# Projecting q and k of one head ahead of a norm, and moving thirty weight subtractions from VectorE to GpSimd

## The chip, the cores and the metric

The kernel runs on one core of one Trainium2 chip. The metric is device time in microseconds (us) for one execution. The engines are TensorE (PE, its weight loads PEld), VectorE (DVE), ScalarE (ACT), GpSimd (POOL) and SyncE (SP), which only issues DMAs here; GpSimd issues some DMAs too.

## What is computed

A decoder trunk of two layers over 512 tokens of width 1024, all in fp32. The mixer runs an S5 state space model (four heads of it, as the kernel groups it) and retention (four heads) side by side, from one projection. Its head matters here:

```python
def rms_norm(x, g):
    xf = x.astype(jnp.float32)
    y = xf * lax.rsqrt(jnp.mean(xf * xf, axis=-1, keepdims=True) + EPS)
    return (y * g.astype(jnp.float32)).astype(x.dtype)
...
for l in range(DEPTH):
    h = rms_norm(x, norm_mix[l])
    proj = h @ w_in[l]
    u, q, k, v, g = jnp.split(proj, split_at, axis=-1)
    y_ssm = s5_mixer(u, ...)
    y_ssm = rms_norm(y_ssm, s5_out_norm[l])
    y_ret = retention(q, k, v, g, positions, ret_out_norm[l])
    x = x + jnp.concatenate([y_ssm, y_ret], axis=-1) @ w_out[l]
    ...
    x = x + memory_cross_attention(h, m, wq, wk, wv, wo)
    ...
    x = x + (jax.nn.silu(h @ w_gate) * (h @ w_up)) @ w_down
return rms_norm(x, norm_final)
```

The row scale of a norm commutes with the projection, so the kernel multiplies x times gain by the weights first and applies the scale (`nrm.bc`) when a result is taken out of PSUM.

## The kernel before

**Precision.** Every large matmul is done as three fp32r matmuls on high and low parts: `mm3` issues high x high, high x low, low x high. The activations' parts are `u_nmh` and `u_nml` in the first norm. Weights come in chunks of 128 x 1024 fp32. For a plain chunk (`prep_chunk`) SyncE loads `raw`, ScalarE copies it to the high part (`w<-raw`, rounded to fp32r), and VectorE writes the low part as raw minus high (`w<-raw,w`). For six chunks of q, k and g in layer 0 the low part is made without VectorE: ScalarE writes minus the high part, and a DMA on GpSimd's queue adds raw to it. Gate and up chunks of the feed-forward go another way (`prep_pair`) and are not touched.

**Order of the weights.** `chunk_order` lists all chunks in the order of their use; for a mixer these are u, then v, then what the string `PLAN[l]` names step by step: Q, K, G project q, k, g of a head; S and Y are the states and the output of an S5 head; C and P the scores and the weighted values of a retention head; M, L, V are memory keys, GLU and memory values; F ends retention. A chunk is prepared when the one four places before it is used (`LOOKAHEAD`); five `raw` and eight `w` buffers turn over.

**Order of the instructions.** The program is recorded first and placed by a list scheduler (`Program.due`, `Program.schedule`) that knows a price for each operation, gives each a due time from its users, and picks on each engine the ready operation with the earliest due time for which buffers are free. `EVAC` bounds how long a result may stay in PSUM before its due time. The result is one fixed order for each engine; all instructions are emitted from one line (L405, memsets from L403). An engine runs its order strictly in turn.

**The first norm (layer 0).** TensorE multiplies u0 and u1 from eight 128 x 256 weight pieces (`u_w0h`, `u_w0l`) as the input x arrives in eight tiles, then u2 and u3 from plain chunks. In the meantime ScalarE squares the tiles (`u_nmq`) and VectorE adds them up (`u_nma`). `nrm.root` then takes the column sum on TensorE (a 128 x 1 matmul, `ps<-c,u_nma`), the inverse root on VectorE, and the spread to all partitions on TensorE (128 x 128 with `ident`). Only then can u leave PSUM, times the scale. The v chunks follow, then `PLAN[0]`, which begins with Q0 K0 S0.

**GpSimd** does the S5 setup of layer 0 at the start (128 x 32 and 128 x 256 operations, ending in `u_s5bb`), clears some buffers with memsets, issues its DMAs and does the last scaling of the kernel. VectorE reads `u_s5bb` for the matrices of S0 (`u_mt`).

Of the kernel before, what the change touches and what calls it, by code (L numbers as in the profile page):

```python
# [38 lines left out]

PLAN = ("Q0 K0 S0 G0 C0 S1 Q1 K1 Y0 P0 S2 G1 Y1 C1 P1 S3 Q2 Y2 K2 Q3 K3 C2 G2 C3 Y3 P2 "  # L40
        "G3 M P3 F L V",
        "Q0 S0 K0 G0 C0 K1 S1 P0 Q1 Y0 G1 C1 S2 Q2 P1 Y1 K2 G2 C2 S3 Y2 Q3 K3 P2 G3 C3 "
        "P3 F M Y3 L V")
EPS = 1e-6
TWO_PI = 6.28318501
# [5 lines left out]

ADDED = ("q", "k", "g")
WARM = 8

# [20 lines left out]
def chunk_order():  # L75

    o = []
    for l in range(L):
        o += [("u", l, m) for m in range(4)]
        o += [("v", l, m) for m in range(4)]  # L80
        count = {"q": 1, "k": 1, "g": 1, "ck": KT, "glu": 2, "cv": 8}
        for step in PLAN[l].split():
            key = {"Q": "q", "K": "k", "G": "g", "M": "ck", "L": "glu", "V": "cv"}.get(step[0])
            if key:
                m = int(step[1:] or 0)
                o += [(key, l, m + i) for i in range(count[key])]
        o += [("out", l, m) for m in range(KT)]
        o += [("cq", l, m) for m in range(KT)]
        o += [("co", l, m) for m in range(KT)]
        for a, b in FPARTS[l]:  # L90
            for f in range(a, b, 2):
                o += [("gate", l, a, b, f), ("up", l, a, b, f)]
            o += [("down", l, f) for f in range(a, b)]
    return o
# [63 lines left out]
class Op:  # L158
    __slots__ = ("i", "prio", "eng", "fn", "args", "dur", "deps", "users", "wait", "ready", "end", "cap",
                 "bufs", "tab", "bytes", "rec")  # L160

# [44 lines left out]
class Program:  # L206
    def __init__(self, slots):
        self.ops, self.slots = [], slots
        self.cap, self.made = CAP, {}

# [9 lines left out]
    def add(self, eng, fn, k):  # L220
        o = Op()
        o.i = len(self.ops)
        o.cap = self.cap
        o.eng, o.fn, o.args = eng, fn, k
# [34 lines left out]
    def due(self):  # L259

        t = 0.0
        for o in self.ops:
            if o.eng == "PE":
                o.prio = t
                t += o.dur
            else:
                o.prio = o.rec = t
        for o in reversed(self.ops):
            if o.eng == "PE":
                o.prio = min([u.prio - o.dur - LEAD for u in o.users if u.eng != "PE"]  # L270
                             + [u.prio for u in o.users if u.eng == "PE"] + [o.prio])
                continue
            o.prio = min([u.prio - o.dur - LEAD for u in o.users] + [o.prio + o.cap])
            o.prio = max(o.prio, o.rec - EARLY)
            if o.bytes:
                o.prio = max(o.prio - AHEAD, FIRST)
            for d in o.deps:
                if d.eng == "PE":
                    o.prio = min(o.prio, d.prio + EVAC)

# [137 lines left out]
def trunk(ctx, tc, io):  # L418
# [48 lines left out]
    for kind in (3, 5):  # L467
        place.update((i, n) for n, i in enumerate(i for i, x in enumerate(order) if len(x) == kind))
    ready = {}
    state = {"prep": 0, "use": 0}  # L470
# [3 lines left out]
    def prep_chunk(i):  # L474
# [9 lines left out]
        else:  # L484
            V.tensor_tensor(out=lo, in0=raw, in1=hi.bitcast(F32), op=sub)
        ready[i] = (hi, lo)
# [150 lines left out]

    vec = load("vec", [P, NVEC])
    xs = [perm([P, SEQ], f"x{i}") for i in range(KT)]
    first = []  # L640
    for i in range(KT):
        Q.dma_start(out=xs[i], in_=io["xT"][:, i, :])
        raw, hi, lo = gen("w0")[:, :256], gen("w0h", F32R)[:, :256], gen("w0l", F32R)[:, :256]
        Q.dma_start(out=raw, in_=io["w"][i // 4, :, 256 * (i % 4):256 * (i % 4) + 256])
# [12 lines left out]
    gam = load("gam", [P, TT * HEADS])  # L657
    geps = load("geps", [P, SEQ])

# [72 lines left out]
    class Norm:  # L732
# [38 lines left out]

        def root(self, wide, scale=1.0):

# [9 lines left out]
            colsum(ps, self.acc, ones_d, nt)  # L783
            self.col = rsqrt(ps[:, :nt], nt, "nrm_col", None, scale)
            pb = bank(self.s + "bc")
            spread(pb, self.col, nt)
# [445 lines left out]

    def proj(key, l, m, nrm):
        ps = bank(key)
        w = chunk(key, l, m)
        for kt in range(KT):
            mm3(ps, cut(w, slice(None), slice(kt * P, (kt + 1) * P)), nrm.parts[kt],
                kt == 0, kt == KT - 1)
        return ps

# [45 lines left out]
    def ret_fin(stat, ys, outs):  # L1286

        m = gen("rm")
        V.tensor_tensor(out=m, in0=stat, in1=geps, op=add)
# [8 lines left out]
    def mixer(l, nrm, nxt, begin):  # L1298
# [12 lines left out]
        if l == 0:  # L1311
            begin()
            pu += [proj("u", l, m, nrm) for m in (2, 3)]
            for x in xs:
                nrm.stat(x)
        nrm.root(False)
        if l == 0:
            rotary()
        cr, sr = gen("cr"), gen("sr")
        V.tensor_tensor(out=cr, in0=rcos, in1=nrm.bc, op=mul)  # L1320
        V.tensor_tensor(out=sr, in0=rsin, in1=nrm.bc, op=mul)
        for m in range(4):
# [4 lines left out]
                            in1=by4(nrm.bc), op=mul)  # L1327
            us.append(u)
        if l == 0:
            selectors()  # L1330
        vs = ret_v(l, nrm)
        mats, sts, zs = {}, {}, {}
# [6 lines left out]

        q, k, p, pg = {}, {}, {}, {}  # L1340
        for step in PLAN[l].split():
# [477 lines left out]
```

## Time and profile before

| | |
|---|---|
| median of 3 runs | 1474.37 us (1473.48 to 1475.53) |
| the profiled execution | 1473.55 us |
| its span, first to last instruction | 1471.7 us |
| mean granted TensorE clock | 0.994 |
| TensorE busy | 1452.0 us, 99% of the span |
| VectorE busy | 1194.9 us, 81% |
| ScalarE busy | 798.8 us, 54% |
| GpSimd busy | 98.7 us, 7% |

Busy time is the sum of an engine's instructions, register and DMA-issuing ones left out. The span lies 1.85 us below the execution's time; the difference is what lies around the instructions. The granted clock is a share of full speed: 1.00 is 2.4 GHz, 0.50 is 1.2 GHz.

### The profile page before, as it was taken

Reading aid. Unit: us, or ns where it says so; the run is one execution under the profiler, and the core shown is the slowest. Engines: PE = TensorE matmul, PEld = TensorE weight load, DVE = VectorE, ACT = ScalarE, POOL = GpSimd, SP = SyncE. Lnnn points to the kernel's source line nnn. Section 1 sums busy time; section 2 is a strip of 40 time slices with the busy share of each in tenths; the row PEclk is TensorE's granted clock in tenths of the full one; section 3 lists DMA queues with packets and bytes.
Section 4 is the critical chain, followed back from the end, with each engine's and each line's share of the span. In section 5 each row is a group of like instructions: output and inputs, shape, how many; then the busy total and the mean of one; then the engine's idle time right before and its main releaser. Section 6 shows DMA issues by size and latency. Waiting matters only on the chain.

```text
span 1471.7 us, 23057 instructions
## 1 busy us (share of the span) xinstructions
PE 1452.0 (99%) x8784; PEld 1277.5 (87%) x8784; DVE 1194.9 (81%) x2078; ACT 798.8 (54%) x1375; POOL 98.7 (7%) x202
## 2 busy tenths in 40 slices
PE   8999999999999999999999999999999999999997
PEld 6888788888898998998988888888889989999897
DVE  8799996676899897897973989757679969869596
ACT  5887665344665464565645436544456636436264
POOL 5721000000000101002000000000000000000001
PEclk8999999999999999999999999999999999999999
DMA  7534534221134334244445553432121322413321
GB/s 254 158 87 105 177 131 154 100 72 51 50 115 149 118 119 151 87 143 156 137 139 170 157 165 115 144 129 87 58 72 57 116 101 87 145 59 127 101 87 58
DMA packets 67311, 172.47 MB, mean 117 GB/s; under 512 B 11264, under 2 KB 22912, under 8 KB 67200
## 3 DMA queue, kind: packets, MB, share of 16 engines
q1 hardware_dynamic: 64096, 160.51, 32.6%
q0 software_dynamic: 3104, 10.49, 2.5%
q8 instruction: 69, 1.13, 0.3%
q14 instruction: 42, 0.34, 0.1%
HBM read 156.55 MB, written 13.63 MB: 116 GB/s over the span
## 4 chain that ended last, share of the span: by engine, by line
PE 81%; DVE 13%; ACT 3%; issue 2%; DMA 0%; SPq 0%; DVEq 0%; ACTq 0%
PE ps L405 81%; DVE w L405 4%; DVE u_gs L405 1%; DVE u_us L405 1%; DVE raw L405 1%; ACT w L405 1%; DVE s L405 1%; DVE u_gw L405 0%; DMA x<-in_xT_dram 0%; ACT u_vc L405 0%; DVE u_actl L405 0%; ACT u_v L405 0%; SPq L405 0%; DVE u_ry L405 0%; DVE u_mt L405 0%
## 5 line engine op out<-in xcount | busy, mean ns | idle before, releaser
L405 ACT ACTIVATE w<-raw 128x1024 fp32r<-128x1024 f32 (+1 forms) x348 | 348.1, 1003 | 415.6 <-PE ps L405 341.6
L405 PE MATMUL ps<-u_nff,w 128*128 128x256 f32 x3696 | 438.6, 279 | 1.0 <-DVE w L405 1.0
L405 PEld LDWEIGHTS ps<-u_nff,w 128*128 128x128 f32 x3696 | 435.8, 188 | 4.4 <-DVE w L405 1.8
L405 DVE TENSOR_TENSOR w<-raw,w 128x1024 fp32r<-128x1024 f32 (+1 forms) x336 | 385.0, 1152 | 54.5 <-ACT w L405 54.1
L405 PE MATMUL ps<-u_acth,w 128*128 128x512 f32 (+1 forms) x768 | 224.1, 374 | 0.0
L405 PEld LDWEIGHTS ps<-u_acth,w 128*128 128x128 f32 x768 | 139.6, 188 | 25.3 <-ACT u_acth L405 0.4
L405 PE MATMUL ps<-u_nmh,w 128*128 128x512 f32 x480 | 158.3, 401 | 0.0
L405 PE MATMUL ps<-u_actl,w 128*128 128x512 f32 (+1 forms) x384 | 143.7, 376 | 1.4 <-DVE u_actl L405 1.2
L405 DVE TENSOR_TENSOR x<-ps,x 128x512 f32<-128x512 f32 x88 | 60.6, 690 | 99.4 <-PE ps L405 99.3
L405 PEld LDWEIGHTS ps<-u_nmh,w 128*128 128x128 f32 x480 | 91.1, 191 | 18.6
L405 PE MATMUL ps<-u_nml,w 128*128 128x512 f32 x240 | 95.4, 397 | 0.0
L405 PEld LDWEIGHTS ps<-u_actl,w 128*128 128x128 f32 x384 | 72.1, 188 | 17.1 <-DVE u_actl L405 3.9
L405 PE MATMUL ps<-u_nch,w 128*128 128x512 f32 x256 | 81.7, 393 | 0.0
L405 PE MATMUL ps<-u_xoh,w 128*128 128x512 f32 x256 | 80.7, 392 | 0.0
L405 DVE TENSOR_TENSOR raw<-raw 128x512 f32<-128x512 f32 x88 | 60.3, 685 | 5.3 <-DMA raw<-in_ws_dram 5.1
L405 DVE TENSOR_TENSOR raw<-raw,raw 128x512 f32<-128x512 f32 x88 | 60.3, 685 | 0.3
L405 DVE TENSOR_TENSOR u_gs<-u_gs,u_nfry 128x512 f32<-128x512 f32 x88 | 59.5, 689 | 0.3
L405 PEld LDWEIGHTS ps<-u_nch,w 128*128 128x128 f32 x256 | 48.1, 188 | 10.4
L405 POOL TENSOR_TENSOR u_fin<-u_lp,u_lbc 128x512 f32<-128x512 f32 x4 | 5.4, 1391 | 767.9 <-ACT u_lbc L405 767.9
L405 PEld LDWEIGHTS ps<-u_xoh,w 128*128 128x128 f32 x256 | 48.0, 188 | 9.9
L405 PEld LDWEIGHTS ps<-u_nml,w 128*128 128x128 f32 x240 | 45.7, 190 | 9.5
L405 PE MATMUL ps<-u_xol,w 128*128 128x512 f32 x128 | 50.4, 393 | 0.0
(368 smaller groups left out, 2472.2 us busy)
## 6 DMA issues: line engine op xcount, KB each, us to landing
raw<-in_w_dram SPq DMA_DIRECT2D x166, 512.0 KB, 3.4
raw<-in_ws_dram SPq DMA_DIRECT2D x88, 512.0 KB, 3.7
u_s5x<-sp SPq DMA_DIRECT2D x28, 256.0 KB, 4.2
w<-in_w_dram POOLq DMA_DIRECT2D x6, 512.0 KB, 6.3
u_mr<-in_memT_dram SPq DMA_DIRECT2D x12, 256.0 KB, 4.7
x<-in_xT_dram SPq DMA_DIRECT2D x8, 256.0 KB, 4.8
tu<-u_u SPq DMA_DIRECT2D x8, 256.0 KB, 3.8
u_ub<-tu SPq DMA_DIRECT2D x32, 64.0 KB, 3.5
```

What stands on the lines that cost most here:

```text
L405: getattr(engines[o.eng], o.fn)(**k)
```

## The change

1. `chunk_order` puts q and k of head 0 of layer 0 between u and v (`AHEAD_OF_NORM`), and `PLAN[0]` loses Q0 K0. In `mixer` the rotary tables are recorded earlier, then q0 is projected, then half of k0; `nrm.root` runs the second half of k0 between its column sum and its spread (`mid`). Both stay in PSUM until the u results are out, and are then rotated. `prog.evac` is 40000 while these steps are recorded and 4000 again after them.
2. `POOLED`: of the list of plain mixer chunks of a layer (u, v, q, k, g, ck, glu, cv: 38 of them), every second from number 13 in layer 0 and from number 4 in layer 1 gets its low part from GpSimd: 13 and 17 chunks.
3. A one-column Copy on ScalarE ahead of everything, and the load of `vec` behind the first tile of x.
4. `geps` is loaded where retention ends, into a passing buffer, and no longer at the start.

```diff
--- before.py
+++ after.py
@@ -37,10 +37,12 @@
 
 
 
-PLAN = ("Q0 K0 S0 G0 C0 S1 Q1 K1 Y0 P0 S2 G1 Y1 C1 P1 S3 Q2 Y2 K2 Q3 K3 C2 G2 C3 Y3 P2 "
+PLAN = ("S0 G0 C0 S1 Q1 K1 Y0 P0 S2 G1 Y1 C1 P1 S3 Q2 Y2 K2 Q3 K3 C2 G2 C3 Y3 P2 "
         "G3 M P3 F L V",
         "Q0 S0 K0 G0 C0 K1 S1 P0 Q1 Y0 G1 C1 S2 Q2 P1 Y1 K2 G2 C2 S3 Y2 Q3 K3 P2 G3 C3 "
         "P3 F M Y3 L V")
+
+AHEAD_OF_NORM = (("q", 0), ("k", 0))
 EPS = 1e-6
 TWO_PI = 6.28318501
 MAGIC = 12582912.0
@@ -50,6 +52,8 @@
 LOOKAHEAD = 4
 
 ADDED = ("q", "k", "g")
+
+POOLED = (13, 4)
 WARM = 8
 
 
@@ -77,6 +81,8 @@
     o = []
     for l in range(L):
         o += [("u", l, m) for m in range(4)]
+        if l == 0:
+            o += [(key, l, m) for key, m in AHEAD_OF_NORM]
         o += [("v", l, m) for m in range(4)]
         count = {"q": 1, "k": 1, "g": 1, "ck": KT, "glu": 2, "cv": 8}
         for step in PLAN[l].split():
@@ -157,7 +163,7 @@
 
 class Op:
     __slots__ = ("i", "prio", "eng", "fn", "args", "dur", "deps", "users", "wait", "ready", "end", "cap",
-                 "bufs", "tab", "bytes", "rec")
+                 "bufs", "tab", "bytes", "rec", "evac")
 
 
 LATENCY = {("PE", "PE"): 0, ("ACT", "ACT"): 0, ("DVE", "DVE"): 127, ("PE", "DVE"): 196,
@@ -206,7 +212,7 @@
 class Program:
     def __init__(self, slots):
         self.ops, self.slots = [], slots
-        self.cap, self.made = CAP, {}
+        self.cap, self.evac, self.made = CAP, EVAC, {}
 
     def buf(self, kind, s="", dt=None):
         b = Buf(kind, None, s)
@@ -220,7 +226,7 @@
     def add(self, eng, fn, k):
         o = Op()
         o.i = len(self.ops)
-        o.cap = self.cap
+        o.cap, o.evac = self.cap, self.evac
         o.eng, o.fn, o.args = eng, fn, k
         o.bytes = 0
         if fn == "dma_start":
@@ -276,7 +282,7 @@
                 o.prio = max(o.prio - AHEAD, FIRST)
             for d in o.deps:
                 if d.eng == "PE":
-                    o.prio = min(o.prio, d.prio + EVAC)
+                    o.prio = min(o.prio, d.prio + o.evac)
 
     def schedule(self):
 
@@ -466,6 +472,13 @@
     place = {}
     for kind in (3, 5):
         place.update((i, n) for n, i in enumerate(i for i, x in enumerate(order) if len(x) == kind))
+
+
+    on_pool = set()
+    for l in range(L):
+        c = [x for x in order if len(x) == 3 and x[1] == l
+             and x[0] in ("u", "v", "q", "k", "g", "ck", "glu", "cv")]
+        on_pool.update(c[POOLED[l]::2])
     ready = {}
     state = {"prep": 0, "use": 0}
 
@@ -482,7 +495,8 @@
             S.activation(out=lo, in_=raw, func=AF.Copy, scale=-1.0)
             G.dma_start(out=lo, in_=io["w"][place[i]].bitcast(F32R), accum_op=add)
         else:
-            V.tensor_tensor(out=lo, in0=raw, in1=hi.bitcast(F32), op=sub)
+            eng = G if order[i] in on_pool else V
+            eng.tensor_tensor(out=lo, in0=raw, in1=hi.bitcast(F32), op=sub)
         ready[i] = (hi, lo)
 
     def chunk(*key):
@@ -635,11 +649,15 @@
         T.matmul(out=ps[:, :P], lhsT=zero[:, :P], rhs=zero[:, :P], start=True, stop=True)
 
 
-    vec = load("vec", [P, NVEC])
+    S.activation(out=zero[:, P:P + 1], in_=zero[:, :1], func=AF.Copy)
+
+
     xs = [perm([P, SEQ], f"x{i}") for i in range(KT)]
     first = []
     for i in range(KT):
         Q.dma_start(out=xs[i], in_=io["xT"][:, i, :])
+        if i == 0:
+            vec = load("vec", [P, NVEC])
         raw, hi, lo = gen("w0")[:, :256], gen("w0h", F32R)[:, :256], gen("w0l", F32R)[:, :256]
         Q.dma_start(out=raw, in_=io["w"][i // 4, :, 256 * (i % 4):256 * (i % 4) + 256])
         S.activation(out=hi, in_=raw, func=AF.Copy)
@@ -655,7 +673,6 @@
     half01 = load("half01", [32, 2])
     tri = load("tri", [P, P])
     gam = load("gam", [P, TT * HEADS])
-    geps = load("geps", [P, SEQ])
 
     def fixed(v):
         x = perm([P, 1], "c")
@@ -769,7 +786,7 @@
                 V.tensor_tensor(out=new[:, :n], in0=self.acc[:, :n], in1=sq[:, :n], op=add)
                 self.acc = new
 
-        def root(self, wide, scale=1.0):
+        def root(self, wide, scale=1.0, mid=None):
 
 
             nt = self.n // P
@@ -782,6 +799,8 @@
             ps = bank(self.s + "cs")
             colsum(ps, self.acc, ones_d, nt)
             self.col = rsqrt(ps[:, :nt], nt, "nrm_col", None, scale)
+            if mid is not None:
+                mid()
             pb = bank(self.s + "bc")
             spread(pb, self.col, nt)
             self.bc = gen(self.s + "b")
@@ -1230,13 +1249,19 @@
             vs.append(vc)
         return vs
 
-    def proj(key, l, m, nrm):
+    def proj_steps(key, l, m, nrm):
+
         ps = bank(key)
         w = chunk(key, l, m)
         for kt in range(KT):
             mm3(ps, cut(w, slice(None), slice(kt * P, (kt + 1) * P)), nrm.parts[kt],
                 kt == 0, kt == KT - 1)
-        return ps
+            if kt == KT // 2 - 1:
+                yield
+        yield ps
+
+    def proj(key, l, m, nrm):
+        return list(proj_steps(key, l, m, nrm))[-1]
 
     def rope(ps, cr, sr, s):
         sw, t1 = gen(s + "w"), gen(s + "t")
@@ -1285,7 +1310,8 @@
 
     def ret_fin(stat, ys, outs):
 
-        m = gen("rm")
+        m, geps = gen("rm"), gen("geps")
+        Q.dma_start(out=geps, in_=io["geps"])
         V.tensor_tensor(out=m, in0=stat, in1=geps, op=add)
         r = split(rsqrt_wide(m, "rr"), "rx")
         for h in range(HEADS):
@@ -1313,9 +1339,15 @@
             pu += [proj("u", l, m, nrm) for m in (2, 3)]
             for x in xs:
                 nrm.stat(x)
-        nrm.root(False)
-        if l == 0:
             rotary()
+            qk = [proj("q", l, 0, nrm)]
+            steps = proj_steps("k", l, 0, nrm)
+            nrm.root(False, mid=lambda: next(steps))
+            qk.append(next(steps))
+        else:
+            nrm.root(False)
+
+        prog.evac = 40000 if l == 0 else EVAC
         cr, sr = gen("cr"), gen("sr")
         V.tensor_tensor(out=cr, in0=rcos, in1=nrm.bc, op=mul)
         V.tensor_tensor(out=sr, in0=rsin, in1=nrm.bc, op=mul)
@@ -1326,8 +1358,11 @@
             V.tensor_tensor(out=u.rearrange("p (s k) -> p s k", s=4), in0=by4(ps),
                             in1=by4(nrm.bc), op=mul)
             us.append(u)
+        q, k, p, pg = {}, {}, {}, {}
         if l == 0:
+            q[0], k[0] = rope(qk[0], cr, sr, "q"), rope(qk[1], cr, sr, "k")
             selectors()
+        prog.evac = EVAC
         vs = ret_v(l, nrm)
         mats, sts, zs = {}, {}, {}
         ys, yr = [None] * 8, []
@@ -1337,7 +1372,6 @@
             mats[h] = s5_setup(l, h, *kvs["ld"]) if l == 0 else s5_fetch(l, h)
             sts[h] = s5_states(l, h, us[h], mats[h])
 
-        q, k, p, pg = {}, {}, {}, {}
         for step in PLAN[l].split():
             h = int(step[1:] or 0)
             step = step[0]
```

**TensorE at the first norm.** Before, from the end of u's matmuls (`ps3` is u2, `ps4` is u3, `w2` and `w3` are u3's high and low part; `ps6<-w4` is the first of v):

```order
L405 MATMUL ps3_119<-u_nmh_381,w1_109 128x512
L405 MATMUL ps4_120<-u_nmh_282,w2_110 128x512
L405 MATMUL ps4_120<-u_nml_287,w2_110 128x512
L405 MATMUL ps5_121<-c_23_151,u_nma_555 128x1 x4
L405 MATMUL ps6_122<-w4_112,u_nmh_282 128x512
L405 MATMUL ps4_120<-u_nmh_282,w3_111 128x512
L405 MATMUL ps4_120<-u_nmh_294,w2_110 128x512
L405 MATMUL ps4_120<-u_nml_303,w2_110 128x512
L405 MATMUL ps4_120<-u_nmh_294,w3_111 128x512
L405 MATMUL ps4_120<-u_nmh_308,w2_110 128x512
```

and now (`ps5<-w4` is q0, `ps6<-w6` is k0, `w5` is q0's low part, which is made by the DMA on GpSimd's queue):

```order
L411 MATMUL ps4_120<-u_nmh_380,w3_111 128x512
L411 MATMUL ps5_121<-u_nmh_282,w4_112 128x512
L411 MATMUL ps5_121<-u_nml_287,w4_112 128x512
L411 MATMUL ps6_122<-u_nmh_282,w6_114 128x512
L411 MATMUL ps7_123<-c_22_150,u_nma_587 128x1 x4
L411 MATMUL ps6_122<-u_nml_287,w6_114 128x512
L411 MATMUL ps6_122<-u_nmh_282,w7_115 128x512
L411 MATMUL ps6_122<-u_nmh_289,w6_114 128x512
L411 MATMUL ps6_122<-u_nml_298,w6_114 128x512
L411 MATMUL ps6_122<-u_nmh_289,w7_115 128x512
L411 MATMUL ps6_122<-u_nmh_304,w6_114 128x512
L411 MATMUL ps6_122<-u_nml_322,w6_114 128x512
```

The column sum (`128x1`) stood behind two matmuls of u3; now all 24 of u3 and three of q0 and k0 stand ahead of it, and q0 and k0 fill the place behind it up to the spread.

**VectorE at the first norm.** Before (`u_nma` are the norm's sums, `w3` is the low part of u3, the `s` rows belong to the S5 setup and the norm's root):

```order
L405 TENSOR_TENSOR u_nma_550<-u_nma_541,u_nmq_432 128x512
L405 SCALAR_TENSOR_TENSOR s29_92<-s29_92,s27_90 128x32
L405 TENSOR_SCALAR phh_32_160<-ph_31_159 128x32
L405 TENSOR_TENSOR u_nma_555<-u_nma_550,u_nmq_439 128x512
L405 TENSOR_SCALAR s29_92<-s29_92 128x32
L405 TENSOR_SCALAR s35_98<-s23_86 128x32
L405 TENSOR_SCALAR phh_32_160<-phh_32_160 128x32
L405 TENSOR_TENSOR w3_111<-raw1_104,w2_110 128x1024
L405 TENSOR_SCALAR s36_99<-ps5_121 128x4
```

and now (`w7` is the low part of k0, `w1` and the second `w3` those of v0 and v1; the last row is the first step of the norm's root):

```order
L411 CAST u_ang_548<-u_angq_272 128x512
L411 TENSOR_TENSOR phl_32_160<-phl_32_160,s27_90 128x32
L411 TENSOR_TENSOR u_nma_554<-u_nma_540,u_nmq_394 128x512
L411 TENSOR_TENSOR w7_115<-raw3_106,w6_114 128x1024
L411 TENSOR_TENSOR u_nma_570<-u_nma_554,u_nmq_418 128x512
L411 TENSOR_TENSOR w1_109<-raw4_107,w0_108 128x1024
L411 TENSOR_TENSOR u_nma_587<-u_nma_570,u_nmq_427 128x512
L411 TENSOR_SCALAR u_ang_548<-u_ang_548,invf_14_142 128x512
L411 TENSOR_SCALAR u_angq_272<-u_ang_548 128x512
L411 TENSOR_TENSOR w3_111<-raw0_103,w2_110 128x1024
L411 TENSOR_SCALAR s37_100<-ps7_123 128x4
```

The low part of u3, which stood behind all sums, now stands eight places ahead of this piece, before the last five sums, and two more low parts stand among the last three sums.

**GpSimd in the mixer of layer 0.** Before, from the last S5 buffers of head 3 on (`u_dt`, `u_car`, `u_cai` are buffers that are cleared):

```order
L403 MEMSET u_dt_1457 128x512
L405 DMA w4_112<-in_w_dram 128x1024
L403 MEMSET u_car_1483 128x512
L403 MEMSET u_cai_1492 128x512
L403 MEMSET u_car_1685 128x512
L403 MEMSET u_cai_1718 128x512
L405 DMA w0_108<-in_w_dram 128x1024
L403 MEMSET u_br_4348 128x512
```

and now:

```order
L411 TENSOR_TENSOR w6_114<-raw0_103,w7_115 128x1024
L409 MEMSET u_dt_1490 128x512
L409 MEMSET u_car_1500 128x512
L409 MEMSET u_cai_1508 128x512
L411 DMA w0_108<-in_w_dram 128x1024
L411 TENSOR_TENSOR w2_110<-raw1_104,w3_111 128x1024
L409 MEMSET u_car_1710 128x512
L409 MEMSET u_cai_1723 128x512
L411 TENSOR_TENSOR w6_114<-raw4_107,w7_115 128x1024
L411 TENSOR_TENSOR w2_110<-raw2_105,w3_111 128x1024
L411 TENSOR_TENSOR w6_114<-raw3_106,w7_115 128x1024
```

Where only memsets and DMA issues stood, subtractions of 128 x 1024 (`w<-raw,w`) stand between them and behind them. Eleven of the thirteen of this layer lie ahead of the GLU norm; the low parts that VectorE makes between the first S5 head's matrices and that norm go from 19 to 8.

## Rows read from the trace of the kernel before

**Rows 1.** The page's part 1: busy us, share of the span, instructions.
```profile
PE 1452.0 (99%) x8784; PEld 1277.5 (87%) x8784; DVE 1194.9 (81%) x2078; ACT 798.8 (54%) x1375; POOL 98.7 (7%) x202
```

**Rows 2.** The page's part 4: the chain that ended last, by engine.
```profile
PE 81%; DVE 13%; ACT 3%; issue 2%; DMA 0%; SPq 0%; DVEq 0%; ACTq 0%
```

**Rows 3.** Windows: us; busy us and instructions per engine; clock, DMA share, GB/s.
```profile
24.00:36.00 12.00, 9.47 (x32) 7.60 (x31) 11.49 (x36) 2.92 (x3) 10.74 (x18) 0.72 0.61 227
69.00:219.00 150.00, 147.83 (x859) 122.53 (x857) 141.67 (x291) 108.55 (x181) 13.18 (x22) 1.00 0.42 125
733.00:942.00 209.00, 207.49 (x1073) 172.97 (x1072) 156.57 (x260) 102.71 (x181) 0.00 (x0) 1.00 0.44 142
```

**Rows 4.** Timeline of TensorE: start us, us, instruction, [idle before <- releaser].
```profile
25.12 0.40 PE L405 MATMUL ps<-u_nml,w 128*128 128x512 f32 x1
28.05 1.87 PE L405 MATMUL ps<-c,u_nma 128*128 128x1 f32 x8 [2.53 <-DVE u_nma L405]
29.78 0.77 PE L405 MATMUL ps<-w,u_nmh 128*128 128x512 f32 x1
30.35 1.05 PE L405 MATMUL ps<-u_nmh,w 128*128 128x512 f32 x2
...
34.19 0.90 PE L405 MATMUL ps<-u_nmh,w 128*128 128x512 f32 x2
34.93 0.39 PE L405 MATMUL ps<-u_nml,w 128*128 128x512 f32 x1
...
37.22 0.39 PE L405 MATMUL ps<-u_nmh,w 128*128 128x512 f32 x1
...
219.12 1.05 PE L405 MATMUL ps<-c,u_gna 128*128 128x1 f32 x8 [0.81 <-DVE u_gna L405]
```

**Rows 5.** Timeline of VectorE around the norm's last sums.
```profile
27.26 0.74 DVE L405 TENSOR_TENSOR u_nma<-u_nma,u_nmq 128x512 f32<-128x512 f32 x1
...
28.19 1.26 DVE L405 TENSOR_TENSOR w<-raw,w 128x1024 fp32r<-128x1024 f32 x1
```

**Rows 6.** Timeline of ScalarE at the start.
```profile
4.25 1.28 ACT L405 ACT_TABLE_LOAD   x1 [4.25 <-DMA x<-in_xT_dram]
...
16.97 0.40 ACT L405 ACTIVATE u_w0h<-u_w 128x256 fp32r<-128x256 f32 x1
```

**Rows 7.** The page's part 6 for GpSimd's queue; timeline of GpSimd in its S5 chain.
```profile
w<-in_w_dram POOLq DMA_DIRECT2D x6, 512.0 KB, 6.3
...
27.54 0.63 POOL L405 TENSOR_SCALAR s<-s 128x32 f32<-128x32 f32 x1
...
66.29 1.84 POOL L405 TENSOR_TENSOR u_s5bb<-u_s5bb,u_s5bt 128x256 f32<-128x256 f32 x1
```

**Rows 8.** VectorE by line and form, 69 to 219 us, then 733 to 942 us.
```profile
L405 DVE TENSOR_TENSOR w<-raw,w 128x1024 fp32r<-128x1024 f32 x19 | 23.1, 1220 | 1.2 <-ACT w L405 1.2
...
L405 DVE TENSOR_TENSOR w<-raw,w 128x1024 fp32r<-128x1024 f32 x33 | 40.2, 1221 | 22.0 <-ACT w L405 21.9
```

**Rows 9.** Timeline of VectorE at the start of the first S5 head.
```profile
74.37 0.69 DVE L405 TENSOR_TENSOR u_kw<-u_kw,u_sr 128x512 f32<-128x512 f32 x1 [3.22 <-ACT u_kw L405]
```

**Rows 10.** Timelines of GpSimd and VectorE at the kernel's last norm.
```profile
1454.07 5.44 POOL L405 TENSOR_TENSOR u_fin<-u_lp,u_lbc 128x512 f32<-128x512 f32 x4 [767.94 <-ACT u_lbc L405]
...
1455.61 1.30 DVE L405 TENSOR_TENSOR u_la<-u_la,u_lq 128x256 f32<-128x256 f32 x1 [0.49 <-ACT u_lq L405]
...
1457.73 0.62 DVE L405 TENSOR_TENSOR u_la<-u_la,u_lq 128x256 f32<-128x256 f32 x1 [0.48 <-ACT u_lq L405]
...
1459.17 0.62 DVE L405 TENSOR_TENSOR u_la<-u_la,u_lq 128x256 f32<-128x256 f32 x1 [0.48 <-ACT u_lq L405]
...
1460.67 0.42 DVE L405 TENSOR_TENSOR u_la<-u_la,u_lq 128x256 f32<-128x256 f32 x1 [0.54 <-ACT u_lq L405]
```

**Rows 11.** Timelines of GpSimd and VectorE near 480 us.
```profile
479.88 0.72 POOL L405 TENSOR_TENSOR u_diag<-s5d,eye 32x256 f32<-32x256 f32 x1
...
480.04 1.65 DVE L405 TENSOR_TENSOR w<-raw,w 128x1024 fp32r<-128x1024 f32 x1
```

## The prediction

> **What bounds the kernel now.** I read the page first, then windows, then the timeline of the engines around the first norm. The page gives TensorE 1452.0 of 1471.7 us of span, VectorE 1194.9, GpSimd 98.7 [rows 1], and the chain that ended last is 81% TensorE, 13% VectorE [rows 2]. So time is won only where TensorE stands idle or runs at its low clock; all its idle time together is 19.7 us. The reader should then see that the places the change touches differ. In 24 to 36 us TensorE is busy 9.47 of 12 us at a granted clock of 0.72 [rows 3]: an idle stretch. In 69 to 219 us (layer 0's mixer from the first S5 head to the GLU norm) TensorE is busy 147.83 of 150 us and VectorE 141.67: both are full. In 733 to 942 us (layer 1's mixer) TensorE is busy 207.49 of 209 us and VectorE 156.57, which leaves VectorE 52 us free [rows 3].
>
> **Part 1: q and k of head 0 ahead of the first norm.** In the timeline TensorE starts a matmul of u3 at 25.12 and the column sum of the norm at 28.05, after 2.53 us without work; what ends the wait is VectorE's last u_nma [rows 4]. Matmuls before had a start every 0.23 us, so the stop costs 28.05 - 25.35 = 2.7 us. Behind it the clock is low: nine matmuls from 30.35 to 34.19 start 0.427 us apart, that is the 1.2 GHz level, and ten from 34.93 to 37.22 start 0.229 us apart, the 2.4 GHz level [rows 4]. With the one ahead of these nine and the two behind them twelve matmuls lie in the slow piece, 12 x 0.2 = 2.4 us lost, and the column sum took 1.87 us against 1.05 us for the one at 219.12 [rows 4], 0.8 us more; with 0.1 us less for the last two, which are half over by then, 3.1 us. Stop and low clock together: **5.8 us**, the most that this part can give.
>
> After the change 25 more matmuls stand ahead of the column sum (the rest of u3 and three of q0 and k0), 25 x 0.229 = 5.7 us of work, twice the stop. What comes in place of the stop: (a) u3's low part. VectorE wrote it at 28.19 to 29.45, behind the norm's sums [rows 5]; it now stands ahead of them, about 2.5 us earlier, so it is ready near 25.7 + 0.2, and TensorE wants it near 24.9: about 0.9 us. (b) That 1.26 us, and two more low parts, now stand before the last u_nma; the sums ended at 28.00 [rows 5], so they end near 32, and TensorE is at the column sum at 25.35 + 0.9 + 5.7 = 31.95; with the step between the engines 0.5 us. (c) q0's low part comes by an accumulating DMA on GpSimd's queue; it stands inside GpSimd's S5 chain, whose rows there run at 27.5 to 28 us [rows 7], and such a transfer lands 6.3 us after its issue [rows 7]: 34 to 35 us, where TensorE wants it nine matmuls behind the column sum, near 35 (0 us, or 1.5 if GpSimd is later; 0.5 taken). The same queue's later S5 work moves back by the one issue and not more. Waits (a) to (c) are each shorter than the 2.5 us stop after which the clock fell, so I take the clock to stay up. Sum: -5.8 + 0.9 + 0.5 + 0.5 = -3.9, taken as **-4 us**; bounds 0 (the waits grow to what is removed) and -6.
>
> What sits behind the waiting column sum is covered: 45 matmuls of q0 and k0, over 10 us, lie between it and v. The rope of q0 and k0 changes place with the first evictions of u on VectorE, the same instructions. **Priced at nothing:** the early table load (its 1.28 us at 4.25 [rows 6] goes ahead of the first norm piece, but the first two chunks are paced by eight weight pieces whose last is converted at 16.97 to 17.37 [rows 6], and this piece comes no earlier); the vec load behind x0 (same cover; without it the first norm piece is later by at most the 4.25 us that ScalarE waits for x0 now [rows 6]); geps loaded later (one DMA on SyncE, wanted only at the end of retention, and cover is the whole mixer).
>
> **Part 2: GpSimd subtracts.** Thirty low parts leave VectorE. One costs VectorE 1.22 us: 19 of them take 23.1 us in 69 to 219 us, 33 take 40.2 us in 733 to 942 us [rows 8]. By the order of the instructions 11 of the 13 in layer 0 lie in the first stretch: VectorE gets 11 x 1.22 = 13.4 us. The price of one on GpSimd is shown by no row; nearest is the final subtraction of the same kind at half the width, 5.44 us for four, or about 1.3 us each once VectorE's share is off [rows 10], so an estimate of 2 x 1.3 = 2.6 us. TensorE needs a chunk every 24 x 0.229 = 5.5 us and four are prepared ahead, so 2.6 us in place of 1.22 us is covered by itself.
>
> What it costs VectorE is the question. While those four ran, VectorE's u_la took 1.30, 0.62 and 0.62 us, and 0.42 us right after them [rows 10]: 0.88 + 0.20 + 0.20 = 1.28 us lost in 5.44, a share of 24%, with VectorE half idle. Upper row: a low part that met a 0.72 us GpSimd instruction took 1.65 us against 1.22 [rows 8, 11], 0.43 of the 0.56 us they shared, about 75%. So one subtraction of 2.6 us holds VectorE up for between 0.24 x 2.6 = 0.6 and 0.75 x 2.6 = 1.95 us; the far ends are 0 and the whole 2.6. Against the 1.22 us removed: VectorE's sum in the stretch moves by 11 x (-0.6 to +0.7) = -7 to +8 us. I take 1.2 us, the middle, since the first row is nearest in operation and size and the second in how full VectorE is: **0 us**, bounds below. The 3.22 us in which VectorE waits for u_kw at 74.37 [rows 9] goes too, because k0 is now projected ahead of v; so VectorE can follow TensorE's 4 us rather than hold them up. In layer 1, 17 subtractions meet 52 us of free VectorE time; TensorE's 1.5 idle us there are all there is to win and a few late evictions all there is to lose: -1 to +3, taken as 0.
>
> The Trainium skill, "SBUF — State Buffer", section "Who interferes with whom", speaks against the change: a VectorE instruction with two SBUF inputs and a GpSimd instruction that reads SBUF exclude each other for the whole instruction, while a VectorE instruction with one SBUF input is free. The trace agrees in kind (two-input u_la held up by 0.88 us, rows 10) but not with the whole length in each case (0.20 us). By that rule the sum would carry 2.6 us a subtraction and come out as in the third case below; by the rows it carries 1.2.
>
> **Sum.** 1473.55 (profiled) - 4 + 0 + 0 = 1469.55; the profiled execution stands 0.82 us below the median of the runs, so **1470.4 us**. 0.2%, which is about what a measurement of this kernel can tell from no change, is 2.95 us: faster is below 1471.4, slower above 1477.3.
>
> **The cases.**
> 1. Forecast, chance 0.42: the head's gain passes on and the mixers are neutral within 1.5 us: 1467 to 1473, point 1470.4.
> 2. VectorE gives the head's gain back, 0.22. For: it is busy 141.67 of 150 us [rows 3], and the GLU norm at 219.12 waited 0.81 us for its u_gna [rows 4]: the end of this stretch is VectorE's. At 1.6 to 1.8 us held up per subtraction its sum grows by 4 to 6 us, most of the 8.3 us it has free, and 2 to 5 us come back on TensorE. Against: it loses the 3.22 us wait. 1471 to 1477.
> 3. Slower, 0.24. Mechanism: in the mixer of layer 0 each subtraction shuts VectorE out for nearly its whole 2.6 us, since almost all that VectorE does there has two SBUF inputs. It decides from 1.22 + 8.3/11 = 1.97 us per subtraction on: then the stretch has no free VectorE time left and is VectorE's length. At 2.6 us: 11 x 1.38 = 15.2 us, less 8.3 free is 7 us longer, and 12 if most of VectorE's waits stay; the head's gain is lost in it, since this stretch begins with work that hangs on GpSimd's S5 chain (its last u_s5bb ends at 66.29 + 1.84 = 68.13 [rows 7]) and not on TensorE. 1478 to 1486. Against: 24% in rows 10, and GpSimd waits for VectorE as well.
> 4. Better, 0.12: a subtraction holds VectorE up for 0.6 us, VectorE gets 7 us, and TensorE's idle 2.2 and 1.5 us in the two mixers [rows 3] go with it: 1470.4 - 3.7, and less if the head gives its whole 5.8: 1464 to 1467. If the change did not do what it says (scheduler puts a subtraction so late on GpSimd that TensorE waits), that is the second case's time.
>
> **How the numbers follow.** Faster: 0.33 of the first case, 0.03 of the second, all of the fourth: 0.48. Same: 0.09 + 0.17 = 0.26. Slower: 0.02 + 0.24 = 0.26. The range reaches from inside the fourth case to the middle of the third, 1464.5 to 1482; about 0.15 is left out. The likeliest case's own range is 1467 to 1473.
>
> **What would show it.** Right: no TensorE wait over 1 us and clock 1.00 in 24 to 36 us; the column sum 3 to 4 us later than 28.05 with no stop before it; 69 to 219 us with eight low parts on VectorE where 19 stood, and its two-input instructions longer beside GpSimd by 1 to 1.5 us per subtraction; everything after the GLU norm shifted by 4 us. Wrong: a clock below 0.9 after the column sum, or a wait for q0's low part of over 2 us (head); VectorE fuller than 95% in 69 to 219 us with TensorE waiting for evictions there, or rows of subtractions of 4 us or more (part 2); a shift that grows between 733 and 942 us (layer 1).

## The result, and the profile after

The changed kernel took 1499.13 us (median of 4, 1498.08 to 1500.28) beside 1473.92 us for the kernel before (median of 4): a ratio of 1.0171, 95% interval 1.0158 to 1.0183, 25 us slower. The forecast of 1470.4 us, its range up to 1482.0 and its likeliest sign were wrong.

The page's part 1 of the changed kernel, which answers to [rows 1]:

```profile
PE 1463.2 (98%) x8784; PEld 1281.6 (86%) x8784; DVE 1203.0 (80%) x2048; ACT 798.7 (53%) x1376; POOL 179.1 (12%) x232
```

VectorE has 30 instructions fewer and is busy 8 us more. TensorE does the same work in 11.2 us more busy time, and its idle time, span less busy, went from 19.7 to 1498.5 - 1463.2 = 35.3 us. 11.2 + 15.6 = 26.8 us is the whole growth of the span. Two questions follow: what makes TensorE idle, and why the same matmuls take longer.

Windows of the changed kernel; the first three lines answer to [rows 3], the others are short stretches behind TensorE's longest stops (columns as there):

```profile
24.00:36.00 12.00, 10.75 (x51) 8.35 (x50) 11.80 (x31) 6.72 (x9) 11.45 (x19) 1.00 1.00 328
69.00:219.00 150.00, 141.64 (x817) 117.13 (x816) 140.65 (x275) 105.25 (x188) 40.00 (x32) 0.98 0.41 119
745.00:958.00 213.00, 205.29 (x1056) 170.54 (x1055) 149.77 (x241) 98.05 (x174) 37.00 (x14) 0.99 0.44 140
...
138.00:142.00 4.00, 4.00 (x15) 3.34 (x14) 4.00 (x8) 2.59 (x3) 0.00 (x0) 0.57 0.56 133
210.00:214.00 4.00, 4.00 (x11) 3.19 (x12) 2.74 (x5) 1.34 (x3) 0.00 (x0) 0.58 0.00 0
227.00:234.00 7.00, 7.00 (x23) 5.84 (x23) 2.63 (x12) 1.06 (x1) 2.35 (x1) 0.51 0.25 75
926.00:931.00 5.00, 3.73 (x12) 3.07 (x13) 3.20 (x6) 1.52 (x3) 0.00 (x1) 0.66 0.35 105
964.00:971.00 7.00, 6.05 (x18) 5.17 (x19) 6.73 (x13) 1.07 (x2) 3.10 (x2) 0.52 0.25 78
```

The head did what it was to do: more matmuls between 24 and 36 us, at full clock. The two mixers lost. TensorE did 817 matmuls in 69 to 219 us where it did 859, and the clock fell to its 1.2 GHz level in five short stretches, three in layer 0's mixer and two in layer 1's; before, neither mixer had one. Matched by their first matmuls, the column sum of layer 0's GLU norm moved from 219.12 to 226.44 (7.3 us later), the feed-forward of layer 0 began 12.3 us later, that of layer 1 25.6 us. From there on 1 us more was lost.

TensorE's longest waits (us in total, times, longest), and in its timeline the one for u_gna, which answers to the last row of [rows 4], and the longest:

```profile
PE ps L411 <- ACT u_rxh L411: 6.5, 2, 4.0
PE ps L411 <- DVE u_gna L411: 4.9, 2, 2.5
PE ps L411 <- DVE u_rsl L411: 2.8, 1, 2.8
...
226.44 1.36 PE L411 MATMUL ps<-c,u_gna 128*128 128x1 f32 x8 [2.40 <-DVE u_gna L411]
...
927.27 1.65 PE L411 MATMUL ps<-u_rxh,pick 128*128 128x512 f32 x3 [4.02 <-ACT u_rxh L411]
```

None of these is a wait for a subtraction of GpSimd. They are waits for chains on VectorE and ScalarE, and the timelines of GpSimd and VectorE ahead of the second one show what had happened to such a chain:

```profile
916.47 2.46 POOL L411 TENSOR_TENSOR w<-raw,w 128x1024 fp32r<-128x1024 f32 x1 [12.12 <-ACT w L411]
923.35 2.65 POOL L411 TENSOR_TENSOR w<-raw,w 128x1024 fp32r<-128x1024 f32 x1 [4.42 <-ACT w L411]
...
916.57 2.90 DVE L411 TENSOR_TENSOR u_ry<-u_ro,u_rg 128x512 f32<-128x512 f32 x1
...
922.52 0.69 DVE L411 SCALAR_TENSOR_TENSOR u_rrt<-u_rrt,u_rm 128x512 f32<-128x512 f32 x1
923.12 0.69 DVE L411 TENSOR_TENSOR u_ksl<-u_kf,u_ksh 128x512 fp32r<-128x512 f32 x1
923.72 2.83 DVE L411 SCALAR_TENSOR_TENSOR u_rry<-u_rrt,u_rry 128x512 f32<-128x512 f32 x1
```

Two instructions took 2.90 and 2.83 us in place of 0.69 us: each began just after a subtraction and ended some 0.55 us behind it. u_rry is a step of retention's root, a serial chain between VectorE and ScalarE whose result is u_rxh; u_ry is not, but it stands between two of the root's steps in VectorE's order. So both hold-ups, 2.2 and 2.1 us, go to the chain's end, and TensorE stood still for 4.02 us. Behind that its clock was low.

### The profile page after: what moved, and what is told of

It is laid out like the page before. It is cut to its first block, busy times and chain, and to the rows that moved or that the text cites. A ratio compares the mean times of both kernels' runs of the same rounds, so it can differ in the third digit from the quotient of the medians.

```text
span 1498.5 us, 23064 instructions
## 1 busy us (share of the span) xinstructions
PE 1463.2 (98%) x8784; PEld 1281.6 (86%) x8784; DVE 1203.0 (80%) x2048; ACT 798.7 (53%) x1376; POOL 179.1 (12%) x232
## 4 chain that ended last, share of the span: by engine, by line
PE 76%; DVE 13%; ACT 3%; issue 2%; DMA 0%; SPq 0%; DVEq 0%; ACTq 0%
PE ps L411 76%; DVE w L411 2%; DVE u_gs L411 1%; DVE u_mt L411 1%; DVE u_us L411 1%; ACT w L411 1%; DVE u_rr L411 0%; DVE u_rry L411 0%; DVE u_gw L411 0%; DVE raw L411 0%; DVE u_zr L411 0%; ACT u_v L411 0%; DVE u_zi L411 0%; DVE u_vr L411 0%; DVE u_actl L411 0%
## 5 line engine op out<-in xcount | busy, mean ns | idle before, releaser
L411 DVE TENSOR_TENSOR w<-raw,w 128x1024 fp32r<-128x1024 f32 (+1 forms) x306 | 351.3, 1155 | 42.3 <-ACT w L411 41.8
L411 POOL TENSOR_TENSOR w<-raw,w 128x1024 fp32r<-128x1024 f32 x30 | 80.6, 2688 | 325.9 <-ACT w L411 280.0
```

The lines of the kernel that those rows point to most:

```text
L411: getattr(engines[o.eng], o.fn)(**k)
```

## The experiments

Theory 1: while GpSimd reads SBUF, VectorE's instructions with two SBUF inputs are shut out; the hold-ups fall into chains that TensorE waits for. Theory 2: the scheduler's new order is the worse one. Theory 3: GpSimd's low parts come late. All ratios are to the kernel before, run in turn with each (its medians were 1474.05 to 1474.80 us).

**Which part.** Head alone:

```diff
-            eng = G if order[i] in on_pool else V
-            eng.tensor_tensor(out=lo, in0=raw, in1=hi.bitcast(F32), op=sub)
+            V.tensor_tensor(out=lo, in0=raw, in1=hi.bitcast(F32), op=sub)
```

> The change without the subtractions on GpSimd (VectorE makes those low parts again); q0 and k0 ahead of the norm stay. If the head gives what the trace of the change shows (the spots behind the norm 2 to 5 us earlier than before, up to the first subtractions), 1468 to 1472 us. If the head's gain is given back on VectorE in the mixer, 1472 to 1476. If the head part is itself a source of the loss, above 1478.

Measured 1473.34 us, ratio 0.9995 (0.9986 to 1.0004): no loss, and no gain that can be told from none. Subtractions alone, the same lines put into the kernel before:

> The kernel before with the same thirty subtractions on GpSimd and nothing else of the change. If the subtractions alone make the loss: 25 us plus the head's 4, so 1497 to 1504 us. If the loss needs both parts together (GpSimd's S5 chain and VectorE more crowded by the head), under 1490.

1498.86 us, 1.0168 (1.0154 to 1.0181). The loss is that of the subtractions, and does not need the head.

**What of the subtractions.** The order kept, GpSimd writing zeros in place of subtracting, so that these low parts are left out of the products:

```diff
+            elif pooled(o):
+                for _ in range(2):
+                    engines["POOL"].memset(k["out"].bitcast(F32), 0.0)
```

(`pooled(o)` stands for the test that `o` is one of the thirty subtractions.)

> The changed kernel in the same order, but GpSimd writes zeros twice over each of the thirty low parts instead of subtracting: about 2 us each on GpSimd, in which it reads nothing from SBUF; the low parts of these thirty chunks are left out of the product. Theory 1, VectorE's two-input instructions are held up by GpSimd's reading: no instruction of VectorE is longer, and the loss goes away, 1464 to 1472 us. Theory 2, the new order is the worse one: stays within 5 us of 1499. Theory 3, the low parts come too late: the zeros depend on nothing and come early, so it also predicts a fall; the next run parts it from theory 1.

1470.90 us, 0.9972 (0.9963 to 0.9982). With GpSimd busy for 1.9 us on average in the place of each subtraction, but reading nothing, the loss is gone. In this kernel's timelines of GpSimd and VectorE the same chain as above runs beside it at its usual length:

```profile
901.89 1.97 POOL L412 MEMSET w<- 128x1024 f32 x2 [3.69 <-PE ps L414]
...
901.76 0.69 DVE L414 TENSOR_TENSOR u_ksl<-u_kf,u_ksh 128x512 fp32r<-128x512 f32 x1
902.36 0.69 DVE L414 SCALAR_TENSOR_TENSOR u_rry<-u_rrt,u_rry 128x512 f32<-128x512 f32 x1
```

```profile
PE 1453.1 (99%) x8784; PEld 1276.1 (87%) x8784; DVE 1164.9 (79%) x2048; ACT 799.0 (54%) x1376; POOL 154.8 (11%) x262
```

VectorE runs the same 2048 instructions here in 1164.9 us (second fence, the page's part 1) as in the changed kernel in 1203.0. The difference, 38.1 us, is what the thirty subtractions held it up: 1.27 us each on the average, against the 1.22 us that each had cost it before. Theory 2 falls as the main cause.

Theory 3, and the order again: VectorE subtracts, at the place where GpSimd's stood.

```diff
+            elif pooled(o):
+                engines["DVE"].tensor_tensor(**k)
```

> The changed kernel in the same order, but each of the thirty subtractions is issued to VectorE at the place in the common order where GpSimd's stood. Theory 1 (GpSimd's reading holds VectorE up): 1469 to 1476 us, since VectorE takes 1.22 us each and nobody is shut out. Theory 2 (the order): 1490 us or more, since the order is the same and VectorE gets 37 us more work. Theory 3 (the low parts too late on GpSimd): 1469 to 1476, as theory 1.

1482.08 us, 1.0053 (1.0039 to 1.0066): outside all three forecasts. Against the head alone, which has the same instructions on every engine, it is 8.7 us slower, so the order does matter: at GpSimd's places VectorE's own 1.22 us stands in the way of the chains as well. At 945.01 us of that trace, for one, it stands between the last two sums of layer 1's GLU norm, whose column sum then waits 1.50 us. The whole change is 17 us slower than this run: that is GpSimd's part. As waits for GpSimd's low parts are absent from TensorE's list in the changed kernel, theory 3 has nothing left to explain.

**How the shut-out works.** Each subtraction cut in four:

```diff
+            elif pooled(o):
+                for c in range(0, 1024, 256):
+                    engines["POOL"].tensor_tensor(out=k["out"][:, c:c + 256], in0=k["in0"][:, c:c + 256],
+                                                  in1=k["in1"][:, c:c + 256], op=k["op"])
```

> The changed kernel in the same order, each subtraction on GpSimd cut into four of 256 columns (0.6 to 0.7 us each). If VectorE is shut out for the length of one GpSimd instruction, no hold-up is longer than 0.7 us and VectorE gets its turn between the quarters; the stops of TensorE stay under 2 us and the clock up: 1478 to 1490 us. If what counts is GpSimd's total reading, the sum held and the time stay: 1495 to 1502.

1491.89 us, 1.0125 (1.0109 to 1.0141), between the two forecasts. The same stretch of the chain in its timelines of GpSimd and VectorE:

```profile
905.85 4.35 POOL L412 TENSOR_TENSOR w<-raw,w 128x256 fp32r<-128x256 f32 x4 [10.37 <-ACT w L415]
...
906.06 1.23 DVE L415 TENSOR_TENSOR u_ry<-u_ro,u_rg 128x512 f32<-128x512 f32 x1
907.21 0.41 DVE L415 TENSOR_TENSOR u_kf<-ps,mem_bc 128x256 f32<-128x256 f32 x1
907.55 0.89 DVE L415 SCALAR_TENSOR_TENSOR u_rrt<-u_rrt,u_rm 128x512 f32<-128x512 f32 x1
908.48 1.12 DVE L415 SCALAR_TENSOR_TENSOR u_rry<-u_rrt,u_rry 128x512 f32<-128x512 f32 x1
```

The two engines now take turns: u_ry loses 0.54 us and not 2.2, but the next ones lose 0.2 to 0.4 us too. VectorE is busy 1194.3 us in all, so it was held up 29.4 us and not 38.1. The stops of TensorE did not stay under 2 us, as the first forecast had it: the longest, 3.3 us at 960.90 us, waits for the root of layer 1's GLU norm, where step after step of 0.16 us took 0.65 beside a quarter, and the clock fell there too. One input in place of two:

```diff
+            elif pooled(o):
+                for _ in range(2):
+                    engines["POOL"].tensor_copy(out=k["out"], in_=k["in0"])
```

> The changed kernel in the same order; in place of each subtraction GpSimd copies the raw chunk twice into the low part (some 1.8 us in all), so that it reads one input and not two, in two instructions; the low parts of these thirty chunks are replaced by the raw chunk. If any reading by GpSimd shuts out VectorE's two-input instructions, these are longer by up to 0.9 us each beside a copy, and the time is between that with zeros (1471) and that of the change (1499), near 1480. If only a second input does, 1469 to 1473, as with zeros.

1489.38 us, 1.0099 (1.0083 to 1.0116): nearer to the change than forecast. VectorE was held up 1189.0 - 1164.9 = 24.1 us by copies that each run 1.04 us undisturbed. So it is reading by GpSimd that shuts VectorE out, with one input as with two.

**Where it costs.** Layer 1 alone, `POOLED = (99, 4)`:

> The change with the subtractions on GpSimd in layer 1 alone (17 of them). The forecast put 0 (-1 to +3) on this part: 1472 to 1477 us. The trace of the change says that the time between the starts of the two feed-forward parts grew by 13.6 us: then 1473.3 (the head alone) + 13.6 = 1485 to 1489.

1489.31 us, 1.0100 (1.0086 to 1.0114), 16 us over the head alone: the second forecast, 0.3 us above its end. Then, of these seventeen, only the eight of v, q, k and g:

```diff
-        on_pool.update(c[POOLED[l]::2])
+        on_pool.update(x for x in c[POOLED[l]::2] if l == 1 and x[0] in ("v", "q", "k", "g"))
```

> The head part, and GpSimd subtracting in layer 1 only the eight chunks of v, q, k and g (v0, v2, q0, g0, q1, q2, g2, k3); the nine of ck, glu and cv back on VectorE. With all seventeen, four of these eight held VectorE up by 1.5 to 2.2 us and TensorE lost 5.6 us up to the last scores of layer 1, 10 to 12 behind them. If the loss goes by the place (what VectorE is held up in), 1474 to 1480 us; if by the number of subtractions, 8/17 of 16 us: 1481.

1476.53 us, 1.0017 (1.0007 to 1.0026): 3 us for eight subtractions, 13 us for the other nine. In the profiles of these two runs the eight held VectorE up for 8.0 us in all and the nine for 13.1 (what the instructions beside them took beyond the usual time of their form), so a microsecond held up cost 0.4 us among the first and 1.0 among the others: the place decides. The nine of ck, glu and cv run beside the serial end of retention and the GLU norm; that VectorE catches up beside the first ones, because TensorE has other work there, is the likely reason and not shown.

**Another way to free VectorE.** All thirty by ScalarE and the accumulating DMA:

```diff
-        if i % 2 == 0 and order[i][0] in ADDED and order[i][1] == 0:
+        if order[i] in on_pool or i % 2 == 0 and order[i][0] in ADDED and order[i][1] == 0:
```

> The change, but the thirty low parts are made the other way that this kernel has: ScalarE writes minus the high part (1 us more each on ScalarE) and a DMA on GpSimd's queue adds the raw chunk. GpSimd reads nothing with its lanes. If sharing SBUF's read side is the whole loss, VectorE's 37 us are saved as with the zeros: 1469 to 1473. If ScalarE's 30 us more or transfers that land 6 us after issue are late for TensorE: 1475 to 1485.

1489.64 us, 1.0108 (1.0090 to 1.0126): a miss of the first forecast, and above the second. The waits of TensorE name the cause, and VectorE's 1161.9 us, 3.0 below the kernel with the zeros, show that GpSimd's DMA issues did not hold it up:

```profile
PE ps L411 <- DMA w<-in_w_dram: 14.8, 6, 5.8
```

Four of these six waits, 13.4 us, lie at chunks of cv and two short ones at ck; none lies at glu. Up to the GLU norm of layer 0 the kernel was 5.5 us ahead of the one before. So only the eight chunks ahead of that (g1, k2, k3, g3, ck1, ck3, ck5, ck7), with the head:

> The head part, and of the thirty low parts only eight of layer 0 (g1, k2, k3, g3, ck1, ck3, ck5, ck7) made with ScalarE and the accumulating DMA; all others on VectorE as before. In the run with all thirty made so, the GLU norm of layer 0 came 5.5 us earlier than in the kernel before (2.8 with the head alone), and its loss lay at six waits for such transfers of glu and cv chunks. If VectorE's end of this mixer is what gave the head's gain back: 1469 to 1471.5 us. If the gain is lost further on, as with the head alone: 1473 to 1474.

1471.90 us, 0.9982 (0.9973 to 0.9991): between the two forecasts, and the one version that computes the whole and is clear of the kernel before, by 0.1 to 0.3%. Its interval and that of the head alone overlap, so that the accumulation adds to the head is likely and not shown.

## Why the prediction was wrong

**The step that failed** is the pricing of part 2 by VectorE's sum: "VectorE's sum in the stretch moves by 11 x (-0.6 to +0.7)", taken as "0 us", and in layer 1 "17 subtractions meet 52 us of free VectorE time", -1 to +3, taken as 0. One term of that sum was too small: for the eleven early subtractions 1.2 us held up each was taken, and they measured 1.86 on average (1.27 over all thirty, since many late ones met nothing that they could hold up). But the sum would have missed the loss with the right term too. 11 x (1.86 - 1.22) is 7.0 us, inside the 8.3 us that VectorE had free, and in the run with layer 1 alone the seventeen held VectorE up 21 us where 20.7 us of its work had left: by the sum neutral, measured 16 us slower. Nor does time go by the sum elsewhere: writing zeros frees 31 us of VectorE against the head alone and wins 2.4 us, and holding VectorE up for 38 us costs 28. What was removed were short pieces that the scheduler had placed with their price known; what came instead were hold-ups of some 2 us that it did not know, inside chains that TensorE waits for. Layer 1's free time covers little of that, because it is not free at the moment of the hold-up; in the profile of the change the price there was 13.3 us from one feed-forward's start to the other's (25.6 - 12.3; the expectation above has 13.6).

**What was missing was the second payment.** Five stops of TensorE, of 2.4 to 4.0 us, each came with a stretch at 1.2 GHz. In the five windows shown above, the clock's shortfall adds up to 11.9 us (0.43 x 4, 0.42 x 4, 0.49 x 7, 0.34 x 5 and 0.48 x 7). The run to set beside it is the head alone, whose clock stayed at 1.00 from the start to 1465 us:

```profile
PE 1451.4 (99%) x8784; PEld 1274.5 (87%) x8784; DVE 1195.8 (81%) x2078; ACT 799.1 (54%) x1376; POOL 96.8 (7%) x202
```

Against its 1451.4 us TensorE is busy 11.8 us longer in the changed kernel, nearly all of it the slow clock, and it is idle for 35.3 us where the head alone has 1471.0 - 1451.4 = 19.6: 11.8 + 15.7 = 27.5 us in all. The 11.2 us against the kernel before are smaller because that one had slow stretches of its own at the start. The prediction had worked out this double price for the one stop that goes (2.7 us of stop, 3.1 us behind it) and did not apply it to stops that could come.

**The third case** had the mechanism and a wrong price. It let the hold-up decide "from 1.97 us per subtraction on", again by the sum, and put its end at 1486 because it left layer 1 out. In layer 0 the eleven early subtractions held VectorE up for 1.44 to 2.18 us each, seven of them below that point, and the GLU norm of layer 0 still came 10 us later than with the head alone (226.44 against 216.32).

**The rule of the Trainium skill** that the prediction set against its rows, "SBUF — State Buffer", section "Who interferes with whom", is what these runs bear out: an instruction of VectorE with two SBUF inputs that begins behind a subtraction waits nearly to its end (2.2 of 2.46 us at 916.57), and one fed from PSUM does not (u_kt at 159.31, in the last section, keeps its 0.69 us beside a subtraction). GpSimd's zeros lengthened none of the 51 two-input instructions beside them by more than 0.03 us. But the page lets an instruction with at most one SBUF input off only outside VectorE's two-port modes, a condition that the prediction left out, and here such instructions were held up, by writes too. In the timelines of GpSimd and VectorE of the kernel with the zeros:

```profile
191.71 2.13 POOL L412 MEMSET w<- 128x1024 f32 x2 [6.42 <-PE ps L414]
...
192.03 0.91 DVE L414 TENSOR_SCALAR u_rry<-u_rm 128x512 int32<-128x512 int32 x1
```

Its usual time is 0.42 us. Three instructions of this operation met the zeros and lost 2.0 us in all, one of them in part beside GpSimd's S5 setup; whether they ran in such a mode no run here shows.

The prediction also misread [rows 10]. The u_la that lost 0.20 us did not meet a weaker lock: the trace has the ends of GpSimd's last three pieces at 1456.63, 1458.07 and 1459.51, and each u_la ended 0.28 us behind one of them. The later two came when little of a piece was left, and so the share of 24% was low.

**Part 1** came out as worked out up to the norm, and then gave its gain back. At 24 to 36 us the clock was 1.00. The timeline of TensorE in the changed kernel, against [rows 4]:

```profile
26.16 0.73 PE L411 MATMUL ps<-u_nmh,w 128*128 128x512 f32 x2 [0.55 <-DVE w L411]
32.85 1.05 PE L411 MATMUL ps<-c,u_nma 128*128 128x1 f32 x8 [0.70 <-DVE u_nma L411]
```

(a) the wait for u3's low part was 0.55 us (0.9 forecast), (b) that for the sums 0.70 us (0.5), (c) q0's low part none (0.5). But of the -4 us the head alone kept 2.8 at the GLU norm of layer 0, 2.2 at that of layer 1 and, over its runs, about 0.7 at the end (1473.3 us). That lies in the second case's range, but not by its mechanism: the lead was 2.9 us at 128 us already and held from there to the norm, whose column sum waited 0.73 us and not 0.81, so VectorE's end of the mixer gave nothing back. Where the first 1 us went, and the small pieces lost in layer 1, no run here shows. The argument that waits under 2.5 us leave the clock up was too simple as well, as the last section shows. The wait for u_kw [rows 9] is gone, as forecast.

## What to carry to other kernels

Do not price a move between VectorE and GpSimd by the two engines' sums, and free time of an engine over a window is no cover: ask which chain each instruction will stand beside, and what waits at the end of that chain. GpSimd reading SBUF beside a VectorE that reads two SBUF inputs was no second engine here but a lock, so its work belongs beside PSUM-fed work or in true gaps. Its writes cost VectorE 2.0 us in thirty places, and its DMA issues nothing that the runs show. And for a kernel whose TensorE is 99% busy, count a new stop twice, once for itself and once for the slow clock that may follow it.

## What the runs showed of the hardware that was not expected

GpSimd can be the one that waits. At 156 us in the changed kernel, it waited through a row of VectorE's two-input instructions and got its turn when one fed from PSUM came; the timelines of GpSimd and VectorE:

```profile
156.22 5.41 POOL L411 TENSOR_TENSOR w<-raw,w 128x1024 fp32r<-128x1024 f32 x1 [20.02 <-ACT w L411]
...
158.71 0.69 DVE L411 TENSOR_TENSOR u_kw<-u_kw,u_sr 128x512 f32<-128x512 f32 x1
159.31 0.69 DVE L411 TENSOR_TENSOR u_kt<-ps,u_cr 128x512 f32<-128x512 f32 x1
159.91 2.26 DVE L411 TENSOR_TENSOR u_ko<-u_kt,u_kw 128x512 f32<-128x512 f32 x1
```

The subtraction takes 2.4 us undisturbed and took 5.41: for 3 us VectorE's back-to-back instructions on SBUF kept their usual 0.69 us. u_kt reads PSUM; the next one, u_ko, found the lock taken and took 2.26 us. So a VectorE that is busy without a gap can hold GpSimd off, here for 3 us, and then pays itself, here 1.57 us. An instruction fed from PSUM is not the only way in: at 923.35, in the timeline of the first section, the subtraction got in between u_ksl and u_rry, which both have two SBUF inputs. What decides that is not shown. A plain one-input copy by GpSimd (1.04 us) had the same effect: in the kernel with the copies a u_rry took 1.52 us in place of 0.69.

The clock fell behind shorter stops than expected, and not behind all of them. In the kernel with the zeros the norm's column sum at 33.09 us waited 1.20 us and the GLU norm's of layer 1 at 938.13 waited 0.59 us, and the clock was low a few us later:

```profile
35.00:39.00 4.00, 4.00 (x12) 3.16 (x11) 4.00 (x15) 0.49 (x1) 3.84 (x7) 0.57 0.73 241
939.00:944.00 5.00, 4.89 (x16) 3.84 (x16) 3.31 (x13) 1.67 (x3) 0.21 (x1) 0.66 0.70 235
```

With the head alone the same column sum waited 0.91 us, and a matmul near 155 us waited 1.8 us for u_sr, and the clock stayed at 1.00 after both. In the kernel with the quarters a stop of 2.02 us at 205.83 left it up and one of 2.01 us at 914.33 did not. What parts these cases stays open here. It bears on the head: a new wait of about 1 us at its column sum can cost part of the 3.1 us that the change saves.
